# Scores by two sets of 64 rows in turn, in one two-bank tile, in the attention of a two-block transformer kernel

## The chip, the cores and the metric

The kernel runs on one NeuronCore of a Trainium2 chip. The metric is device time in microseconds (us), the median of the runs. The core has TensorE (PE, the matmuls; PEld are its weight loads), VectorE (DVE), ScalarE (ACT), GpSimdE (POOL) and SyncE (SP, which issues the DMAs). [...] Matmuls write to PSUM, which has eight banks of 128 partitions x 512 fp32.

## The reference, cut to what matters

The first block is a two-layer transformer on 512 tokens, the second block a single layer. The change lies in the attention of the first block, which has two kinds, run one after the other in each layer:

```python
# differential attention, 8 heads, two score sets of 64 features per head
sc = einsum('bhcqd,bhckd->bhcqk', q, k) * 64 ** -0.5     # c = 0, 1
p = softmax(sc)
w = p[:, :, 0] - lam * p[:, :, 1]
o = einsum('bhqk,bhkd->bhqd', w, v)                      # v: 128 features

# dilated windows, 3 groups x 4 heads of 64 features
sc = where(valid, q @ k^T * 64 ** -0.5, -1e30)
p = softmax over the keys of all three groups of a head  # joined by their log-sum-exp
o = p @ v                                                # v: 64 features
```

All inputs are fp32. Products are kept near fp32 by splitting a number into a high part in a shorter format (F32R) and a low part, the rest; a product is then hi*hi + hi*lo + lo*hi.

## The kernel before, in words

Each layer's `attention` is a list of six parts: four of kind A (differential, two heads `hl` each, parts j = 0 to 3) and two of kind B (dilated, two heads each, `half` 0 and 1). Part i+1 is projected (`project_a`, `project_b`) after part i's attention in program order, so projections and attention can run side by side. A scheduler sets the order on each engine by a cost model of its own and by priority in program order; the kernel pins a few instructions with `keep_in_program_order` (behind the matmul traced just before) and `issue_after`. q, k and v tiles have two buffers each, so a part's projection can be two parts ahead, not more.

Kind A: the score tile of 128 queries x 512 keys is made per head, query tile `qt` and set c. A set has 64 features, half of the array's rows. `stack` (L466 to L478) therefore lays q_hi and q_lo one above the other in 128 rows (`qst`), and k_hi twice (`kst`), so one full matmul (L495) gives hi*hi + lo*hi; a second one with 64 rows (L498) adds q_hi * k_lo (`tg`). The maximum (L536), the exponential (L539), the weighted difference (L544, L545), four transposes into a `ta` bank (L548), a copy to `wT` (L550) and four value products into the bank `pv` (L552) follow. The two sets' score tiles are two separate buffers of the tag `sc`, one bank each.

Kind B: per row block r (4) and head h (2), the scores of group 0 are made as in A (L609, L610) and those of groups 1 and 2 by two plain fp32 matmuls of 64 rows (L613) into a second `sc` bank. Mask adds (L616, L617), maximum, exponential (L622), scaling (L624), six transposes (L629) into two `ta` banks, two copies (L630, L631) and six value products (L635, 64 columns wide, into partitions 64h to 64h+63 of `pv`) follow. A plain fp32 matmul shows as two passes in the trace, an F32R one as one.

PSUM in the attention: `mm` 2 banks (projections), `tr` 1, `sc` 2, `ta` 2, `pv` 1. Around B half 1, four calls of `gates` (projections of the gate, two output tiles of 24 matmuls each) are traced early; two are free, two are held behind `self.b_ins[1]` and `[2]`, the last value products of r = 1 and r = 2.

## Time and profile before

| | before |
|---|---|
| median of 3 runs | 3705.43 us (3701.24 to 3707.47) |
| the profiled execution | 3702.62 us, span 3700.8 us |
| PE busy | 3565.2 us, 96% of the span |
| DVE / ACT / POOL busy | 71% / 42% / 21% |
| kind A attention of layer 0 | 109.85 to 354.7 us |
| kind B attention of layer 0 | 354.7 to 514.2 us |

The same two stretches of layer 1 run from 1075 to 1472 us. In a timeline row the first number is a start, the second how long the merged instructions took. A matmul's shown duration holds its pipeline's filling, so what one costs is the distance from its start to the next start. "64*128 64x512" is a matmul that uses 64 rows and 128 columns of the array on a moving operand of 512.

### The profile page before, as it was taken

To read this page: it belongs to the slowest core of one execution; us is meant where nothing else is said; L and a number is where in the kernel's file an instruction comes from. 1 tells how busy PE (TensorE), PEld (TensorE's weight loads), DVE (VectorE), ACT (ScalarE), POOL (GpSimd) and SP (SyncE) were. 2 spreads that over 40 slices of the span, in tenths; PEclk is the share of its full clock that TensorE was granted. 3 is DMA by queue.
4 is the path that set the end of the run, shared out by engine and by line. 5 is a ranking of instruction groups with operands and counts; after the bars stand their busy time and mean duration, and the time that the engine had idled before them with its cause. 6 is when DMAs were issued, how large, how long until landed. Compare 5 with 4: busy or idle time off the path is not lost.

```text
span 3700.8 us, 53078 instructions
## 1 busy us (share of the span) xinstructions
PE 3565.2 (96%) x19035; PEld 3036.2 (82%) x19035; DVE 2629.2 (71%) x6192; ACT 1558.3 (42%) x3041; POOL 781.3 (21%) x890
## 2 busy tenths in 40 slices
PE   6999999999999999999999999999998999999998
PEld 5888877988887888898887867899997888888887
DVE  7777568785378764468854575369999887777777
ACT  4566543423256654243243464433554333333332
POOL 4322200200142320020012220131101223333333
PEclk9999999999999999999999999999999999999999
DMA  5111247573321112345751111555455998888887
GB/s 194 64 41 52 69 134 258 173 248 123 110 78 46 56 45 66 100 158 191 241 162 59 54 55 41 164 171 171 159 201 199 335 332 291 299 301 292 297 300 277
DMA packets 228821, 611.33 MB, mean 165 GB/s; under 512 B 24070, under 2 KB 89638, under 8 KB 225868
## 3 DMA queue, kind: packets, MB, share of 16 engines
q1 hardware_dynamic: 191692, 473.69, 38.0%
q0 software_dynamic: 36864, 134.23, 10.8%
q8 instruction: 150, 2.46, 0.3%
q14 instruction: 115, 0.94, 0.1%
HBM read 566.66 MB, written 41.18 MB: 164 GB/s over the span
## 4 chain that ended last, share of the span: by engine, by line
PE 63%; DVE 15%; DMA 14%; ACT 4%; issue 3%; POOL 1%; DVEq 0%; ACTq 0%; SPq 0%; POOLq 0%
PE mm L124 14%; PE mm L125 14%; PE mm L126 14%; DMA raw<-uT 8%; DMA raw<-v 5%; DVE wlo L118 5%; ACT whi L117 3%; PE pv L552 2%; PE sc L498 1%; DVE oi L1770 1%; PE pv L635 1%; DVE adaj L229 1%; DVE oj L1762 1%; PE mm L1772 1%; PE sc L495 1%
## 5 line engine op out<-in xcount | busy, mean ns | idle before, releaser
L117 ACT CAST whi<-raw 128x1024 fp32r<-128x1024 f32 (+2 forms) x603 | 610.0, 1015 | 1160.0 <-DMA raw<-uT 398.8
L118 DVE TENSOR_TENSOR wlo<-raw,whi 128x1024 fp32r<-128x1024 f32 (+2 forms) x583 | 689.4, 1185 | 460.8 <-ACT whi L117 401.1
L126 PE MATMUL tr<-hhi,wlo 128*128 128x384 f32 x1024 | 353.8, 346 | 27.1 <-DVE wlo L118 27.0
L124 PE MATMUL mm<-hhi,whi 128*128 128x512 f32 (+1 forms) x976 | 365.9, 375 | 0.2 <-ACT mr L743 0.2
L125 PE MATMUL mm<-hlo,whi 128*128 128x512 f32 (+1 forms) x976 | 363.8, 373 | 1.8 <-DVE hlo L153 1.2
L126 PE MATMUL mm<-hhi,wlo 128*128 128x512 f32 (+1 forms) x976 | 363.9, 373 | 0.0
L124 PE MATMUL tr<-hhi,whi 128*128 128x384 f32 x1024 | 350.3, 342 | 13.8 <-ACT whi L117 10.7
L125 PE MATMUL tr<-hlo,whi 128*128 128x384 f32 x1024 | 347.2, 339 | 0.0
L124 PE MATMUL mm<-whi,hhi 128*128 128x384 f32 (+2 forms) x896 | 310.3, 348 | 18.7 <-ACT hhi L152 13.7
L125 PE MATMUL mm<-wlo,hhi 128*128 128x384 f32 (+2 forms) x896 | 310.8, 347 | 3.2 <-DVE wlo L118 3.2
L229 DVE CUSTOM_DVE_ANT_0 adaj<-adaw,cr 128x256 f32<-128x256 f32 x620 | 272.0, 439 | 58.7 <-DMA adaw<-ada_w 45.0
L126 PE MATMUL mm<-whi,hlo 128*128 128x384 f32 (+2 forms) x896 | 308.1, 344 | 0.0
L282 POOL TENSOR_TENSOR nsum<-nsum,nsq 128x256 f32<-128x256 f32 x78 | 68.6, 883 | 1114.5 <-ACT nsq L280 1113.0
L1845 POOL DMA_INDIRECT raw<-u,idx x128 | 148.4, 1159 | 457.3 <-DVE act L1853 315.2
L126 PEld LDWEIGHTS tr<-hhi,wlo 128*128 128x128 f32 x1024 | 194.1, 190 | 44.6 <-DVE wlo L118 43.6
L124 PEld LDWEIGHTS tr<-hhi,whi 128*128 128x128 f32 x1024 | 194.3, 190 | 26.9 <-ACT whi L117 21.1
L125 PEld LDWEIGHTS mm<-hlo,whi 128*128 128x128 f32 x976 | 183.8, 188 | 34.4 <-DVE hlo L153 1.6
L126 PEld LDWEIGHTS mm<-hhi,wlo 128*128 128x128 f32 x976 | 183.7, 188 | 32.9 <-issue 0.4
L124 PEld LDWEIGHTS mm<-hhi,whi 128*128 128x128 f32 x976 | 183.5, 188 | 32.5 <-issue 0.6
L124 PEld LDWEIGHTS mm<-whi,hhi 128*128 128x128 f32 x896 | 170.9, 191 | 38.4 <-ACT hhi L152 13.8
L125 PE MATMUL mm<-wlo,ewh 128*128 128x512 f32 x512 | 200.9, 392 | 0.0
L126 PE MATMUL mm<-whi,ewl 128*128 128x512 f32 x512 | 199.9, 392 | 0.0
(604 smaller groups left out, 8410.5 us busy)
## 6 DMA issues: line engine op xcount, KB each, us to landing
adaw<-ada_w SPq DMA_DIRECT2D x139, 512.0 KB, 4.4
raw<-uT SPq DMA_DIRECT2D x128, 512.0 KB, 4.6
raw<-v SPq DMA_DIRECT2D x128, 512.0 KB, 5.5
raw<-w_up SPq DMA_DIRECT2D x64, 512.0 KB, 4.3
raw<-w_dn SPq DMA_DIRECT2D x64, 512.0 KB, 3.6
raw<-w_b SPq DMA_DIRECT2D x48, 384.0 KB, 3.5
raw<-w_aqk SPq DMA_DIRECT2D x32, 512.0 KB, 3.7
raw<-w_g SPq DMA_DIRECT2D x32, 512.0 KB, 4.3
```

The costliest lines, as they stand in the source:

```text
L117: nc.scalar.copy(hi[:, :n], raw[:, :n])
L118: self.last_lo = (eng or nc.vector).tensor_sub(lo[:, :n], raw[:, :n], hi[:, :n])
L124: mm(ps, ah, bh, start=start, stop=False)
L125: mm(ps, ah, bl, start=False, stop=False)
L126: mm(ps, al, bh, start=False, stop=stop)
L229: nc.vector.tensor_tensor_reduce(junk, wt[:, q * 256 : q * 256 + 256], cond[:, q * 256 : q * 256 + 256], op0=ALU.mult, op1=ALU.add, scale= ...
L282: add_ins = (nc.vector if k == 7 else nc.gpsimd).tensor_add(tot, tot, sq)
L495: self.nc.tensor.matmul(ps, q(c, slice(0, P)), k(c), start=True, stop=False)
L498: self.nc.tensor.matmul(ps, q(c, r), k(2)[r], start=False, stop=True)
L552: nc.tensor.matmul(po[:, cols], wT[:, kt], v[:, kt, hl * P : hl * P + P], start=(kt == 0), stop=(kt == 3))
L635: ins = nc.tensor.matmul(po[rows, cols], v[:, kt, g * P + 64 * h : g * P + 64 * h + 64], wT[:, k, :], start=(k == 0), stop=(k == 5))
L1845: nc.gpsimd.indirect_dma_start(z, None, src, bass.IndirectOffsetOnAxis(ap=idx[:, k % P : k % P + 1], axis=0))
```

## The change

`stack`, `stack_one` and `stacked` go. `parts_of` makes the high and the low part of q and of k over all 128 partitions (set or head 0 in partitions 0 to 63, set or head 1 in 64 to 127), with one ACT and one DVE instruction. `three` lists the three 64-row products hi*hi, hi*lo, lo*hi of a score, and `by_turns` issues those of the two sets (A) or heads (B) alternately, each pinned behind the one before. The two scores of a turn lie in the two halves of one two-bank tile `pair` that has a single buffer, where there were two tiles of one bank. In B, both heads of an r go together: their scores, then the plain products of groups 1 and 2 (into `ta` banks now), later the value products of both heads alternately, once both `wT` are there.

```diff
     def attention_banks(self):
-        self.banks(mm=2, tr=1, sc=2, ta=2, pv=1)
+        self.banks(mm=2, tr=1, pair=1, ta=2, pv=1)
...
+        if tag == "sc" and "pair" in self.nbanks:
+
+            if not self.second_half:
+                self.second_half = [self.t(self.pm, [P, 2, 512], "pair")]
+                return self.second_half[0][:, 0]
+            return self.second_half.pop()[:, 1]
...
+    def by_turns(self, *products):
+
+        n = len(products[0])
+        for k in range(n):
+            for p, step in enumerate(products):
+                ins = self.nc.tensor.matmul(*step[k][:3], start=step[k][3], stop=step[k][4])
+                if k or p:
+                    self.tc.keep_in_program_order(ins)
+        return ins
+
+    def parts_of(self, hi, lo, src, gain):
+
+        self.nc.scalar.activation(hi, src, AF.Copy, scale=gain)
+        self.nc.vector.scalar_tensor_tensor(lo, src, gain, hi, ALU.mult, ALU.subtract)
+
+    def three(self, ps, q, k):
+
+        return [(ps, q[0], k[0], True, False), (ps, q[0], k[1], False, False), (ps, q[1], k[0], False, True)]
...
-                self.stacked(pss, lambda c, r: q[c][r, hl, cols], lambda c: k[c][:, hl])
+                self.by_turns(*(self.three(ps, [z[64 * c : 64 * c + 64, hl, cols] for z in q],
+                                           [z[64 * c : 64 * c + 64, hl] for z in k]) for c, ps in enumerate(pss)))
...
-            for h in range(2):
+            cols = slice(r * P, r * P + P)
+            pss = [(self.sc_ps(), self.bank("ta")) for _ in range(2)]
+            steps = []
+            for h, (ps, p2) in enumerate(pss):
                 rows = slice(64 * h, 64 * h + 64)
...
+                steps.append(self.three(ps, [qT[0][rows, i, cols] for i in range(2)], [kT[0][rows, i] for i in range(2)]))
+                steps[h] += [(p2[:, g * P : g * P + P], qT[1][rows, g, cols], kT[1][rows, g, cols], True, True)
+                             for g in range(2)]
+            self.by_turns(*steps)
...
+            ins = self.by_turns(*([(po[64 * h : 64 * h + 64, cols], v[:, k if k < 4 else r, 64 * (h + 2 * max(k - 3, 0)) :][:, :64],
+                                    wT[:, k, :], k == 4, k == 3) for k in (4, 5, 0, 1, 2, 3)] for h, wT in reversed(list(enumerate(wTs)))))
             self.b_ins = (self.b_ins if r else []) + [ins]
```

What the scheduler makes of it on PE, at the end of part j = 1 of kind A in layer 0, `hl` 1. Before (L495 and L498 are scores, `ta` transposes, `mm` projections):

```order
L495 MATMUL sc_1784<-kst_291_1186,qst_289_1184 128x512
L498 MATMUL sc_1784<-tg_1188,qst_289_1184 128x512
L125 MATMUL mm_2667<-wlo_2502,hhi_438 128x512
L495 MATMUL sc_1785<-kst_292_1187,qst_290_1185 128x512
L498 MATMUL sc_1785<-tg_1188,qst_290_1185 128x512
L563 MATMUL ta_1681<-ident_72,osb_1671 128x128 x4
L548 MATMUL ta_1709<-ident_72,p_1703 128x128 x4
L126 MATMUL mm_2667<-whi_2501,hlo_446 128x512
L124 MATMUL mm_2667<-whi_2501,hhi_439 128x512
L125 MATMUL mm_2667<-wlo_2502,hhi_439 128x512
L126 MATMUL mm_2667<-whi_2501,hlo_447 128x512
L124 MATMUL mm_2734<-whi_2724,hhi_432 128x256
```

And now, at the same part and head (L479 is `by_turns`, L541 the transposes, L545 the value products):

```order
L541 MATMUL ta_1671<-ident_72,p_1665 128x128 x4
L479 MATMUL pair_1716<-kst_281_1168,qst_279_1166 128x512 x2
L479 MATMUL pair_1716<-kst_282_1169,qst_279_1166 128x512 x2
L479 MATMUL pair_1716<-kst_281_1168,qst_280_1167 128x512 x2
L545 MATMUL pv_1649<-v_1386,wT_1676 128x128 x4
L541 MATMUL ta_1703<-ident_72,p_1697 128x128 x4
L545 MATMUL pv_1649<-v_1386,wT_1708 128x128 x4
L479 MATMUL pair_1748<-kst_281_1168,qst_279_1166 128x512 x2
L479 MATMUL pair_1748<-kst_282_1169,qst_279_1166 128x512 x2
L479 MATMUL pair_1748<-kst_281_1168,qst_280_1167 128x512 x2
L541 MATMUL ta_1735<-ident_72,p_1729 128x128 x4
L545 MATMUL pv_1649<-v_1386,wT_1740 128x128 x4
```

The projections that stood between the attention's steps have moved ahead of this place; here scores, transposes and value products follow each other with no projection between them, up to the next transposition of a projection (`tr`) and its matmuls.

On PE in kind B of layer 0, half 1, before (L635 are value products, `mm_4915` is a gate's projection):

```order
L124 MATMUL mm_4915<-hhi_432,whi_4911 128x512
L635 MATMUL pv_4538<-wT_4555,v_4409 64x128 x6
L629 MATMUL ta_4589<-ident_72,p_4578 128x128 x4
L629 MATMUL ta_4590<-ident_72,p_4578 128x128 x2
L609 MATMUL sc_4638<-kst_872_4183,qst_834_3965 128x512
L610 MATMUL sc_4638<-tg_3124,qst_834_3965 128x512
L613 MATMUL sc_4641<-kst_873_4184,qst_835_3966 128x128 x2
L125 MATMUL mm_4915<-hlo_440,whi_4911 128x512
L126 MATMUL mm_4915<-hhi_432,wlo_4912 128x512
```

And now, from the last value products of half 0 on (`pair_4559` are scores of half 1's r = 2, `ta_4426`, `ta_4427` and `ta_4493` plain products of its r = 0 and 1, L621 the transposes of its r = 0):

```order
L479 MATMUL pv_3604<-wT_3850,v_3475 64x128
L479 MATMUL pv_3604<-wT_3829,v_3475 64x128
L479 MATMUL ta_4427<-kst_831_4086,qst_793_3876 128x128
L479 MATMUL ta_4426<-kst_831_4086,qst_793_3876 128x128
L479 MATMUL ta_4427<-kst_831_4086,qst_793_3876 128x128
L479 MATMUL pair_4559<-kst_830_4085,qst_792_3875 128x512 x6
L621 MATMUL ta_4449<-ident_72,p_4438 128x128 x4
L621 MATMUL ta_4450<-ident_72,p_4438 128x128 x2
L621 MATMUL ta_4470<-ident_72,p_4459 128x128 x4
L621 MATMUL ta_4471<-ident_72,p_4459 128x128 x2
L479 MATMUL ta_4493<-kst_831_4086,qst_793_3876 128x128
L479 MATMUL pv_4424<-wT_4469,v_4295 64x128
```

The transposes of an r now stand right behind its plain products and the next scores, and the next r's plain products stand behind those transposes, since both use the two `ta` banks; the gates' projections stand before and after this stretch. The same two patterns stand in layer 1.

## Rows read from the trace of the kernel before

**Rows 1.** Busy time by stretch: kinds A and B, layer 0; then PEclk, DMA share, GB/s.

```profile
109.85:354.70 244.85, 244.33 (x1401) 200.18 (x1400) 191.35 (x457) 153.54 (x376) 77.45 (x107) 1.00 0.16 50
354.70:514.20 159.50, 159.50 (x918) 134.46 (x917) 84.72 (x168) 73.26 (x149) 23.68 (x41) 1.00 0.21 68
```

**Rows 2.** Chain of waits in kind B, 354.7 to 514.2 us, shares by line.

```profile
by line: PE mm L126 20.4%; PE mm L124 20.3%; PE mm L125 20.3%; PE pv L635 15.0%; PE ta L629 8.4%; PE sc L613 5.1%; PE sc L610 4.3%; PE sc L609 2.3%; PE tr L588 1.8%; PE pv L552 1.7%; PE ta L548 0.3%; PE ta L563 0.3%
```

**Rows 3.** Timeline of PE around one score of kind A: start, us, engine, line.

```profile
109.61 0.40 PE L126 MATMUL mm<-whi,hlo 128*128 128x512 f32 x1
109.85 0.39 PE L495 MATMUL sc<-kst,qst 128*128 128x512 f32 x1
110.17 0.49 PE L498 MATMUL sc<-tg,qst 64*128 64x512 f32 x1
110.59 0.50 PE L124 MATMUL mm<-whi,hhi 128*128 128x512 f32 x1
110.92 0.40 PE L125 MATMUL mm<-wlo,hhi 128*128 128x512 f32 x1
```

**Rows 4.** Timeline of PE where both sets' 64-row scores stand together, layer 1.

```profile
1136.60 0.49 PE L498 MATMUL sc<-tg,qst 64*128 64x512 f32 x2
1137.02 0.44 PE L511 MATMUL tr<-ident,qs 128*128 128x128 f32 x2
```

**Rows 5.** Timeline of PE in the second block, four plain products of 64x64, two passes each.

```profile
2093.13 0.66 PE L1479 MATMUL lm<-va,kw 64*64 64x129 f32 x8
```

**Rows 6.** Timeline of PE around the scores of one head of kind B.

```profile
472.61 0.50 PE L610 MATMUL sc<-tg,qst 64*128 64x512 f32 x1
472.94 0.60 PE L613 MATMUL sc<-kst,qst 64*128 64x128 f32 x4
473.48 0.50 PE L126 MATMUL mm<-hhi,wlo 128*128 128x512 f32 x1
```

**Rows 7.** Timeline of PE, value products of one head of kind B.

```profile
424.89 1.52 PE L635 MATMUL pv<-wT,v 128*64 128x128 f32 x12
```

**Rows 8.** Groups by line: one of the low parts in `stack`, DVE.

```profile
L476 DVE SCALAR_TENSOR_TENSOR qst<-tr,gcol,qst 64x256 fp32r<-64x256 f32 x26 | 12.6, 483 | 9.4 <-ACT kst L475 8.7
```

**Rows 9.** One line's instructions in kind A: duration ns min/median/max, first and last start.

```profile
L536 DVE TENSOR_REDUCE mx<-sc x128: 673/692/694, 110.9 to 1309.9; 128x1 f32<-128x512 f32 x128
L539 ACT ACTIVATE p<-sc,mx x128: 668/688/704, 112.5 to 1311.5; 128x512 f32<-128x512 f32 x128
L544 DVE TENSOR_SCALAR p<-p,s x64: 473/480/561, 117.9 to 1312.6; 128x512 f32<-128x512 f32 x64
L545 DVE SCALAR_TENSOR_TENSOR p<-p,s,p x64: 741/751/836, 119.4 to 1313.1; 128x512 f32<-128x512 f32 x64
L550 ACT COPY wT<-ta x64: 572/586/603, 126.8 to 1317.8; 128x512 f32<-128x512 f32 x64
```

**Rows 10.** Timeline of all engines, softmax of one head of kind B.

```profile
494.53 0.38 ACT L631 COPY wT<-ta 128x256 f32<-128x256 f32 x1
...
494.85 0.42 DVE L617 TENSOR_TENSOR p<-sc,mask 128x256 f32<-128x256 f32 x1 [2.87 <-PE sc L613]
...
495.31 0.95 DVE L619 TENSOR_REDUCE bmx<-p 128x1 f32<-128x768 f32 x1
495.31 0.39 PE L125 MATMUL mm<-hlo,whi 128*128 128x512 f32 x1
...
495.54 0.40 PE L126 MATMUL mm<-hhi,wlo 128*128 128x512 f32 x1
...
496.48 0.94 ACT L622 ACTIVATE p<-p,bmx 128x768 f32<-128x768 f32 x1 [1.58 <-DVE bmx L620]
...
497.74 0.62 DVE L624 TENSOR_SCALAR p<-p,bsum 128x768 f32<-128x768 f32 x1
```

**Rows 11.** Busy time by stretch around a wait of PE in the first projections.

```profile
60.30:63.80 3.50, 0.34 (x2) 0.00 (x0) 3.46 (x12) 0.92 (x1) 0.00 (x0) 1.00 0.25 74
63.89:67.30 3.41, 3.41 (x8) 2.69 (x9) 1.89 (x3) 1.14 (x2) 0.00 (x0) 0.50 0.58 180
```

## The prediction, made before the result was known

> **What bounds the kernel now.** I read the busy times by stretch first. In kind A of layer 0 PE is busy for 244.33 of 244.85 us, DVE for 191.35 (78%), ACT for 153.54; in kind B PE for all 159.50, DVE for 84.72 [rows 1]. The reader is to see that PE has no gap in either stretch, so what a score or value product costs on PE is paid in full, and what DVE or ACT does beside it is not. The chain of waits in B says the same: every share is PE's, the projections' three lines 61%, and the lines that the change touches (L609, L610, L613, L635) 2.3 + 4.3 + 5.1 + 15.0 = 26.7%, 42.6 us a layer [rows 2]. Then I read starts in the timeline to price a single score, and last the order on PE before and after, because a stretch that is full can only lose time if work stops lying beside the waits of the softmax.

> **PE work, kind A.** From the starts [rows 3]: a full score matmul is 0.32 to the next start (109.85 to 110.17), the 64-row one 0.42 (110.17 to 110.59), and the projection after it 0.33. Among projections alone it is 0.23 (495.31 to 495.54) [rows 10]. So the changes of shape cost 0.09, 0.19 (of which 0.11 is taken as a weight load that nothing hides, as the one behind shows) and 0.10, together 0.38, and a set costs two matmuls of 0.23 and that, 0.84; 1.68 a turn of two sets. After: six 64-row matmuls. Two 64-row matmuls that stand together take 0.42 to the next start (1136.60 to 1137.02), as long as one alone [rows 4]: the two sets use different halves of the rows and run side by side. So the turn costs 3 x 0.23 + 0.38, some 1.08; saved 0.60. There are 2 layers x 4 parts x 2 heads x 4 query tiles = 64 turns: **-38**. The other end: if they ran one after the other, 6 x 0.23 + 0.38 = 1.76, which is +5. I take the first, since rows 4 show that very pair.

> Whether the second and third pass of a set can load their weights while the set's own rows still work: four passes over the same 64 rows take 0.60, less 0.27 of emptying (what a matmul's shown 0.50 has over 0.23), so they stand 0.11 apart [rows 6], no further than twelve value products over all rows (1.52 less 0.27, over eleven) [rows 7]. I take no open load. [...]

> **PE work, kind B.** Per row block r and head: L609 0.32 as in A, L610 0.33 (472.61 to 472.94), L613 0.54 (472.94 to 473.48), and 0.11 on the matmul behind: 1.30 [rows 6]. Value products: twelve passes in 1.52 shown, 1.31 from the first to the next work's start (1.25 and one hand-over), and some 0.3 for the changes of shape around them [rows 7]. That is 2.9 a head, 5.8 for the two; the chain's 42.6 us over 8 row blocks is 5.3, which leaves out what the neighbours pay. After: scores 1.08, plain products of both heads side by side 4 x 0.11, together 1.5; value products of both heads by turns in 12 slots, 1.31, and 0.6 for changes: 3.4. Saved 2.4 x 16 (2 layers x 2 halves x 4) = **-38**. That half-column products of two heads run side by side is not shown here. The nearest row is of 64x64 passes: eight took 0.66 [rows 5], where one after the other would be 7 x 0.11 + 0.27 = 1.04. So pairs do run together. If the value products did not, 1.31 x 16 = 21 comes back.

> **Stacking.** Per 128 tokens of q and k, four ACT instructions, four low parts of 483 ns [rows 8] and two copies become two and two. Neither engine is the bound in A or B, and PE work lies over it, so nothing; the DMAs are the same. It matters only as room on DVE, rival 1.

> **What the order takes away.** PE now stands bare in some turns: no projection lies between a turn's steps. In B there are three such turns a layer (half 0's r = 3, half 1's r = 0 and 1), and r = 2 of half 0 has only fourteen projections (14 x 0.23 = 3.2 us). Their chain, with durations from [rows 10], from the last plain product on: 0.27 of emptying, two adds of 0.42, two maxima of 0.95 with 0.22 for the small operation and the hand-over behind each, the second exponential 0.94, 0.32 to the scaling, 0.62. The first head's scaling is squeezed in at about 4.2, its transposes (six at 0.11, and 0.27 of emptying) and copies (0.59 [rows 9], 0.38) end at 6.2. The `ta` banks are only two, and the plain products use them now as well: so the second head's transposes wait for those copies, the next r's plain products for the second head's copies (8.2), and with value products and plain products the turn closes at about 10.3. PE works for 1.1 (next scores) + 1.3 (transposes) + 1.3 to 1.6 (value products) + 0.4, some 4.5 in all; 5.8 idle. Per layer 3 x 5.8, 2.6 at the r with fourteen projections, and 1.3 (transposes' emptying and two copies) at each of the two last turns: 22.6, both layers **+45**. Behind the waiting transposes on PE stand the value products, the next scores and the gates' projections; all wait.

> In A the order has bare turns at the end of parts j = 0 (one), 1 (three) and 2 (three). `pair` has a single buffer, so the next scores wait for both exponentials. Chain of a turn, [rows 9] for durations: two maxima of 0.69 and their 0.2, exponential 0.69 and 0.19 for its sum, 0.47 for two small operations, 0.48, 0.75: 4.4. PE works for 1.08 + 0.44 + 0.44 and 0.4 of changes of shape, 2.4. So 2.0 idle in 7 turns, and at the end of each of three stretches a copy that the value products wait for (0.71 of transposes + 0.59): 18 a layer, **+36**. The ends: no idle at all, if the exponentials and DVE's steps of successive turns overlap fully, and 5.0 a turn (idle 2.6) if the copy to `wT` always stands ahead of the second exponential: 0 and 46.

> **Clock.** [...] The bare turns in B have one wait of about 3.1 us each: six, at some 1.4 us: **+8**; nothing at one end, 20 at the other, if the clock stays low through the whole of them.

> **Sum.** -38 - 38 + 45 + 36 + 8 = +13 on the profiled 3702.6 (the span 3700.8 and 1.8 around it): 3716. The median of the runs shown is 2.8 above the profiled one, so 3718.

> **Rivals.**
> 1. The other side: the A turns are not bare in effect. DVE without stacking has 3.3 us of work in a turn (2 x 0.84 + 0.48 + 0.75 + 0.33); if softmax steps of neighbouring turns overlap, a turn takes that, its idle is 0.8, and A's waits are 7 x 0.8 x 2 = 12 instead of 36: 3694. It decides from a turn under 3.5 us on, for then A wins more than B loses. For it: DVE is the next busiest engine in A and it gets lighter. Against: single-buffered `pair`. With B's turns also a quarter shorter, 3680.
> 2. Longer waits: the clock stays half through the bare stretches (+12) and an A turn takes 5.0 (+10, with the stretches' ends a little more): 3718 + 25 = 3743. For it: in B 3.1 us waits follow each other at 10 us. Against: between them PE works without a break for some us.
> 3. The change does not do what it says. Either each further pass over the same rows pays an open load of 0.11 [rows 3]: two in each of A's 64 turns, 14 us, and five in each of B's 16 row blocks, 9 us: 3741. Or the turns run one after the other: serial scores alone bring 44 in A, 3762; serial value products alone 21, 3739. Against: [rows 4 to 6]. [...]

> **How the numbers follow.** Forecast 0.50, with its own range 3696 to 3740 (waits of 81 us, give or take a quarter, and a little for the PE terms); rival 1 0.25; rival 2 0.17; rival 3 0.08 (0.05 for open loads, 0.03 for serial turns). A difference of 0.2%, 7.4 us, is about what a measurement of this kernel can tell from no change: 3698 to 3713. Of the forecast's half, 0.30 lies above 3713, 0.15 within, 0.05 below; rival 1 gives 0.22 faster and 0.03 within; rivals 2 and 3 are slower, but for 0.01. Faster 0.27, same 0.19, slower 0.54. The range takes in rival 1 from 3675 and rival 2 to 3750.

> **What would show it.** In the timeline of A, six L479 in about 1.08 us with starts in pairs, and in B value products of both heads starting in pairs; starts 0.23 apart singly would mean rival 3. Waits of PE of about 3 us ahead of L621 in B's bare turns, released by DVE's scaling, and of 1.3 ahead of the second head's, released by ACT's copy; a granted clock under 1.00 there. Stage B longer than its 159.5 us and A near its 245. I am wrong if A falls under 235 (rival 1) or if B, waits and all, stays under 155.

## The result, and the profile after

| | before | changed |
|---|---|---|
| median | 3705.8 us (3701.2 to 3707.5) | 3748.0 us (3746.8 to 3748.9) |
| ratio, 95% interval | | 1.0116 (1.0098 to 1.0133) |
| span of the profiled run | 3700.8 us | 3747.0 us |
| PE / DVE / ACT busy | 96% / 71% / 42% | 94% / 68% / 41% |

The changed kernel is 42 us slower. Each engine has less work than before; PE's 3541 us of it are spread over a span that is 46 us longer.

What the change was to save is there. The timeline of PE around one turn of kind A, in the kernel after (it answers to [rows 3]):

```profile
198.54 0.39 PE L131 MATMUL mm<-whi,hhi 128*128 128x512 f32 x1
198.86 0.98 PE L479 MATMUL pair<-kst,qst 64*128 64x512 f32 x6
199.76 0.50 PE L132 MATMUL mm<-wlo,hhi 128*128 128x512 f32 x1
```

Six passes take 0.90 us from their first start to the next work's, where the two sets took 1.56 before (49.8 us in layer 0 over 32 turns); their starts come in pairs (198.86, 199.20 and 199.44, twice each). What is new are waits of PE in an attention that had next to none [rows 1, 2]. Waits of PE in layer 0's attention, after (us in total, times, longest):

```profile
PE ta L621 <- DVE p L615: 10.9, 4, 3.7
PE pv L545 <- ACT wT L543: 5.5, 7, 1.2
PE mm L131 <- ACT sq L455: 3.7, 3, 1.5
PE ta L479 <- ACT wT L622: 2.7, 5, 1.3
PE pair L479 <- ACT p L532: 2.3, 2, 1.2
PE ta L621 <- ACT wT L622: 1.9, 4, 1.1
PE pv L479 <- ACT wT L623: 1.6, 1, 1.6
```

B's own (L621, L479 on `ta` and `pv`) sum to 17.1 us, A's (with 1.5 at `tr` and 1.4 at L541) to 10.7; the 3.7 ahead of projections (L131) were 0.5 in this layer before. In layer 1 each of these rows is the same within 0.5. Timeline of one bare turn of B, after, some rows left out:

```profile
452.17 0.48 PE L479 MATMUL ta<-kst,qst 64*128 64x128 f32 x2 [0.51 <-ACT wT L622]
452.59 2.76 PE L479 MATMUL pv<-wT,v 128*64 128x128 f32 x24
...
456.13 0.93 PE L479 MATMUL pair<-kst,qst 64*128 64x512 f32 x5
456.80 1.80 DVE L610 TENSOR_REDUCE bmx<-p 128x1 f32<-128x768 f32 x2
...
460.72 1.51 PE L621 MATMUL ta<-ident,p 128*128 128x128 f32 x6 [3.65 <-DVE p L615]
...
462.48 1.54 PE L621 MATMUL ta<-ident,p 128*128 128x128 f32 x6 [0.25 <-ACT wT L622]
...
464.33 0.79 PE L479 MATMUL ta<-kst,qst 64*128 64x128 f32 x2 [0.30 <-ACT wT L622]
```

The turn takes 12.16 us (452.17 to 464.33). The wait of 3.65 us for the softmax stands where the prediction put it, but what stands beside it is slow: six transposes take 1.51 us, and the 24 value products 2.76 here and 2.83 behind the wait (at 465.05), where those of an undisturbed turn take 1.53 (at 477.36). The granted clock says why: it was 0.52 from 452.59 to 455.40, and 0.50 from 459.60 to 469.70. Busy times by stretch (PE, PEld, DVE, ACT, POOL), then PEclk, DMA share, GB/s, after:

```profile
448.00:470.00 22.00, 15.83 (x103) 12.23 (x101) 10.89 (x22) 8.11 (x17) 0.00 (x0) 0.69 0.06 24
470.00:505.00 35.00, 26.95 (x154) 21.56 (x154) 14.70 (x33) 11.62 (x25) 0.00 (x0) 0.80 0.06 16
```

Where the time goes, by events that all kernels have (us later than in the kernel before; "layer 0's outputs" is the last matmul on `ohi` there, the last of the attention's output projection, "second block" its last `mm<-hhi,whi`, "end" the last matmul), with the median and its ratio of the kernels run. Each row's events are read from one profiled execution, which can lie several us off its median (5.6 above it for b_only, 5.5 below for after_fill). The kernels are those of the next section:

| | layer 0's outputs | layer 1's outputs | second block | end | median | ratio (interval) |
|---|---|---|---|---|---|---|
| changed | +7.2 | +27.8 | +36.3 | +47.5 | 3748.0 | 1.0116 (1.0098 to 1.0133) |
| two_sc | -0.4 | +9.0 | +9.6 | +24.6 | 3724.4 | 1.0054 (1.0037 to 1.0071) |
| a_only | -5.2 | -6.5 | -6.3 | -3.1 | 3699.7 | 0.9990 (0.9979 to 1.0002) |
| b_only | 0.0 | +12.8 | +16.5 | +26.6 | 3722.2 | 1.0047 (1.0030 to 1.0064) |
| serial | +12.2 | +42.0 | +42.1 | +46.5 | 3749.3 | 1.0125 (1.0107 to 1.0143) |
| after_fill | -2.4 | +11.0 | +13.5 | +14.6 | 3721.7 | 1.0043 (1.0029 to 1.0056) |
| after_warm | -1.4 | +14.6 | +16.6 | +20.4 | 3720.9 | 1.0039 (1.0020 to 1.0057) |
| after_qr | +6.6 | +29.6 | +32.0 | +38.7 | 3745.0 | 1.0110 (1.0090 to 1.0130) |
| by_turns_fill | -8.6 | -6.2 | -5.8 | -2.7 | 3703.9 | 1.0000 (0.9981 to 1.0018) |
| b_fill2 | -12.7 | -13.1 | -13.2 | -7.1 | 3695.3 | 0.9974 (0.9963 to 0.9986) |
| by_turns_fill2 | -17.7 | -22.9 | -22.5 | -19.0 | 3687.4 | 0.9959 (0.9946 to 0.9971) |
| a_rev | -7.1 | -10.3 | -9.8 | -2.9 | 3700.6 | 0.9994 (0.9981 to 1.0006) |

So 28 us of the loss arise in the first block, 8.5 in the second block's attention and 11 in the experts' part behind it, which goes on to the end and whose code is the same.

### The profile page after: what moved, and what is told of

Its sections match the earlier page's. It is cut to its first block, busy times and chain, and to the rows that moved or that the text cites. A ratio compares the mean times of both kernels' runs of the same rounds, so it can differ in the third digit from the quotient of the medians.

```text
span 3747.0 us, 53123 instructions
## 1 busy us (share of the span) xinstructions
PE 3540.9 (94%) x19195; PEld 3034.0 (81%) x19195; DVE 2565.4 (68%) x6000; ACT 1518.4 (41%) x2945; POOL 775.2 (21%) x890
## 4 chain that ended last, share of the span: by engine, by line
PE 61%; DVE 15%; DMA 15%; ACT 5%; issue 3%; POOL 1%; SPq 0%; DVEq 0%; ACTq 0%; POOLq 0%
PE mm L132 14%; PE mm L131 14%; PE mm L133 14%; DMA raw<-uT 8%; DVE wlo L125 5%; DMA raw<-v 3%; ACT whi L124 3%; PE pair L479 2%; PE pv L545 1%; DVE oi L1759 1%; PE mm L1761 1%; DVE ewl L160 1%; DMA act<-actd 1%; PE tr L133 1%; PE tr L131 1%
## 5 line engine op out<-in xcount | busy, mean ns | idle before, releaser
L131 PE MATMUL tr<-hhi,whi 128*128 128x384 f32 x1024 | 353.0, 345 | 15.7 <-ACT whi L124 10.2
L131 PE MATMUL mm<-hhi,whi 128*128 128x512 f32 (+1 forms) x976 | 366.0, 375 | 0.2 <-ACT mr L732 0.2
L131 PE MATMUL mm<-whi,hhi 128*128 128x384 f32 (+2 forms) x896 | 308.1, 345 | 24.8 <-ACT hhi L159 14.7
L131 PEld LDWEIGHTS tr<-hhi,whi 128*128 128x128 f32 x1024 | 196.4, 192 | 29.4 <-ACT whi L124 21.5
L131 PEld LDWEIGHTS mm<-hhi,whi 128*128 128x128 f32 x976 | 183.8, 189 | 32.5 <-ACT mr L732 0.4
L131 PEld LDWEIGHTS mm<-whi,hhi 128*128 128x128 f32 x896 | 170.7, 191 | 41.5 <-ACT hhi L159 15.0
```

The source lines that it names most:

```text
L131: mm(ps, ah, bh, start=start, stop=False)
```

## The experiments

**Which half of the change costs: two_sc, a_only, b_only.** In two_sc `pair` gives way to two buffers of one bank; a_only and b_only are the kernel before with one kind's functions exchanged.

```diff
-        self.banks(mm=2, tr=1, pair=1, ta=2, pv=1)
+        self.banks(mm=2, tr=1, sc=2, ta=2, pv=1)
```

> The changed kernel with the two-bank tile `pair` replaced by two tiles of one bank each (tag sc, two buffers, as before the change); scores and value products still go by turns. Theory (waits that the order leaves bare cost the time): the order now puts projections between all but 2 of the 64 turns of kind A, so A's extra idle of about 15 us a layer and the 4 us at the next layer's first outputs go, while kind B keeps its three bare turns a layer: 3690 to 3705. Rival (the time goes to the matmuls by turns themselves, or to code after the attention): 3735 to 3750.

> The kernel before with only kind A's scores by turns (two sc tiles of one bank, kind B as before). Theory: A's scores fall from 49.8 to about 30 us a layer, no bare turns are added in A or B, so 35 to 40 us are gained: 3665 to 3680. Rival (by turns itself brings waits to A): 3700 or more.

> The kernel before with only kind B changed (both heads together, plain products in the ta banks, value products by turns; two sc tiles of one bank, kind A as before). Theory: B saves about 13 us of PE work a layer, and its bare turns cost about 18 us of waits and 8 us of halved clock a layer: 3725 to 3740. Rival (all of the loss comes from the two-bank tile with its single buffer): 3675 to 3685.

Measured at layer 1's outputs: two_sc +9.0, a_only -6.5, b_only +12.8. The single buffer of `pair` therefore costs 19 us net, about half of what the theory put on it (15 a layer and 4), and B's half loses even without it. The medians still miss: two_sc by 20 us, 15 of which arise behind the second block's attention, b_only by 3 on the lower side, and A's half by 20, -6.5 instead of -35. With two banks the six passes of a turn rarely stand together. In two_sc, timeline of PE:

```profile
191.96 0.28 PE L133 MATMUL mm<-whi,hlo 128*128 128x256 f32 x1
192.17 0.50 PE L479 MATMUL sc<-kst,qst 64*128 64x512 f32 x1
192.60 0.39 PE L131 MATMUL mm<-whi,hhi 128*128 128x256 f32 x1
...
193.74 0.96 PE L479 MATMUL sc<-kst,qst 64*128 64x512 f32 x5
```

One pass goes alone and pays its change of shape (0.43 here), and the other five pay theirs (0.96 shown for five, where 0.98 are shown for six together); that this is because the first bank comes free ahead of the second is argued here, and a_rev tests it. From start to next start, a pass costs 0.211 us in a_only and 0.158 with `pair`: 40 us a layer in A against 30, after 50 before. The two-bank tile keeps the passes together and pays for it with waits. Nor does a_only keep the 10 us a layer that its scores save: in layer 0 its projections of 384 and 256 columns cost 2.8 us more than before, and A's transposes and value products 3.4 more; that this comes from the passes of another shape that they now stand next to is the author's reading.

**Does the first set matter: a_rev.** a_only with `reversed(list(enumerate(pss)))` in the call of `by_turns`.

> a_only with set 1 issued ahead of set 0 in each turn, so that fewer first passes stand alone between projections (34 turns of 64 split 1 and 5 in both, 25 runs of six instead of 16). Theory (a turn's six passes cost 0.21 us each with two banks and 0.16 with one two-bank tile because the first pass goes alone and pays its change of shape twice): a few us less than a_only, 3690 to 3698. Rival (the split does not matter): 3700.

The scores fall from 40.4 to 38.4 us a layer and layer 1's outputs come 4 us earlier than in a_only; 3700.6 against 3699.7 does not show it, since the trace loses it again in the experts' part: as the theory has it in the trace, inconclusive in the median.

**Does the alternation matter: serial.**

```diff
-        for k in range(n):
-            for p, step in enumerate(products):
+        for p, step in enumerate(products):
+            for k in range(n):
```

> The changed kernel with by_turns issuing all steps of the first set or head and then all of the second; the same matmuls, not alternated. Theory (two sets run side by side only when they alternate): 0.7 to 0.8 us more in each of 64 turns of A, 0.8 + 1.3 in each of 16 of B, some of it within the bare waits: 3790 to 3830. Rival (PE pairs neighbours in any order, or the alternation does nothing): 3748, as the changed kernel.

The median is that of the changed kernel, the rival's number, but by chance: at layer 1's outputs serial is 14 us later, and it gets that back because its second block does not lose the 8.5 us and its end loses less. The price per product was mis-expected all the same. Timeline of PE in serial, a turn of A and B's value products:

```profile
200.09 0.98 PE L479 MATMUL pair<-kst,qst 64*128 64x512 f32 x6
201.01 0.50 PE L132 MATMUL mm<-wlo,hhi 128*128 128x512 f32 x1
...
458.65 2.45 PE L479 MATMUL pv<-wT,v 128*64 128x128 f32 x24
```

Six score passes queued set by set still take 0.92 us, and A's scores cost 31.5 us a layer for 30.3. What grows are the 24 value products, from 1.53 (at the full clock, below) to 2.45 (granted clock 1.00).

**Waits against clock: after_fill and after_warm.** after_fill holds each output tile of the first four gates behind the value products of a row block (`self.b_ins` now keeps all eight of a layer); after_warm adds work.

```diff
-            for m, r in enumerate((None, None, 1, 2)):
+            for m, held in enumerate(((1, 2), (3, 4), (4, 5), (6, 6))):
```

```diff
+            if self.nth_b % 2 and r:
+                steps = [[(*z[0][:4], True)] * 12 + z for z in steps]
```

> The changed kernel with the eight output tiles of the first four gates' projections (24 matmuls, 5.5 us each) held one by one behind the value products of kind B's row blocks, so that projections stand in each of its formerly bare turns; kind A and the rest as in the changed kernel. Theory (bare turns: some 18 us of waits and 7 of halved clock a layer in B): 30 to 40 us less, 3708 to 3720, and a granted clock of 1.00 in that stretch. Rival (these waits only move to another place): 3740 to 3750.

> The changed kernel with work added: in half 1 of kind B, row blocks 1 to 3, the first score pass of both heads is issued 12 times more before the three that count (2.8 us more matmuls at the full clock in each of six turns, all ahead of the wait of 4 us for the softmax; the result is unchanged, since the last pass with start overwrites). Theory (the halved clock after the wait is a cost of its own, some 3 us a turn): the added passes hide in the wait, transposes and value products run at the full clock, 3725 to 3738. Rival (only the waits cost, the clock plays no part on this chain): 3746 to 3750. Third (the added passes themselves run at the half clock): 3755 to 3765.

after_warm is the plainest result of the study: 144 matmuls more, and 27 us less. 16 us of that lie in the two layers' attention (8.6 and 7.7, by the events; 3 of them are lost again behind layer 0's attention), 6 in the second block, the rest behind it. The same turn in after_warm:

```profile
452.56 0.48 PE L480 MATMUL ta<-kst,qst 64*128 64x128 f32 x2 [0.51 <-ACT wT L626]
452.98 1.53 PE L480 MATMUL pv<-wT,v 128*64 128x128 f32 x24
...
454.91 3.67 PE L480 MATMUL pair<-kst,qst 64*128 64x512 f32 x29
...
459.58 0.85 PE L625 MATMUL ta<-ident,p 128*128 128x128 f32 x6 [1.00 <-DVE p L619]
...
462.27 0.48 PE L480 MATMUL ta<-kst,qst 64*128 64x128 f32 x2 [0.51 <-ACT wT L626]
```

and its stretches:

```profile
448.00:470.00 22.00, 17.08 (x158) 13.35 (x156) 13.88 (x29) 10.51 (x24) 0.00 (x0) 1.00 0.08 25
470.00:505.00 35.00, 30.76 (x226) 24.96 (x225) 16.41 (x36) 13.47 (x28) 0.00 (x0) 1.00 0.07 20
```

The added passes fill the wait (1.00 is left of 3.65), the granted clock stays at 1.00, six transposes take 0.85 instead of 1.51, the value products 1.53 instead of 2.76, and the turn 9.71 instead of 12.16. The clock is a cost of its own, about as large as the theory said (2.5 us a turn for 3); the total gained more than expected, through the second block and what lies behind it. after_fill gains 17 us at layer 1's outputs, half of what was expected, and its median misses the range by 2: it left one turn bare (a wait of 5.9 us at 421 us, with a granted clock of 0.82 in 420 to 448 us), and the second heads' waits of 1.3 stayed.

**The second block: after_qr.**

```diff
+                with self.after(*(self.ropes[-3:-2] if (t, d) == (0, 1) else [])):
+                    for h in range(4):
+                        nc.scalar.activation(dm[:, h], dm[:, h], AF.Exp, bias=m[:, h : h + 1])
```

> The changed kernel with one order pinned in the second block: the first token tile's two rope copies (ACT, qR) stand ahead of the second direction's exponentials (dm), as they did in the kernel before. Theory (8 us of the loss are this order, which the scheduler's model of time shifted, and the half clock behind the wait of 2.0 us): 3738 to 3742, and the stretch from the second block's first lm matmul to its last mm<-hhi,whi about 386 us instead of 395. Rival (the clock falls there anyhow): 3746 to 3750.

In the changed kernel ACT has the copies to `qR` behind the exponentials of `dm`, where the kernel before has them ahead. Timeline of PE there, after, and then the same matmuls in after_qr and before:

```profile
2183.63 0.48 PE L1320 MATMUL th<-kTr,qR 64*128 64x256 f32 x1 [1.99 <-ACT qR L1224]
...
2198.86 2.07 PE L1319 MATMUL ms<-kTn,qT 128*128 128x512 f32 x2
2200.87 2.07 PE L1320 MATMUL ms<-kTr,qR 64*128 64x512 f32 x2
```

```profile
2185.13 0.48 PE L1321 MATMUL th<-kTr,qR 64*128 64x256 f32 x1 [1.72 <-ACT qR L1225]
...
2198.06 1.13 PE L1320 MATMUL ms<-kTn,qT 128*128 128x512 f32 x2
2199.12 1.12 PE L1321 MATMUL ms<-kTr,qR 64*128 64x512 f32 x2
```

```profile
2166.43 1.13 PE L1330 MATMUL ms<-kTn,qT 128*128 128x512 f32 x2
2167.49 1.12 PE L1331 MATMUL ms<-kTr,qR 64*128 64x512 f32 x2
```

From the first `lm<-whi,chi` matmul to the last `mm<-hhi,whi` it is 394.8 us after, 388.7 in after_qr, 386.4 before. The half clock of the later matmuls went with the order, 6 of the 8 us: the granted clock was 0.50 from 2193.50 to 2207.15 after, and 1.00 in after_qr from 2193.00 to 2206.70. The wait itself shrank little (1.99 to 1.72), so that this wait alone made the clock fall is not shown. Other kernels agree on the order: in two_sc and serial the copies to `qR` stand ahead of those exponentials, and they lose 0.6 and 0.1 us in this block. The median moved by 3 us, to between the two forecasts, and the two kernels' ranges overlap: confirmed in the stretch, not shown in the whole.

**A version that keeps the gain: by_turns_fill, b_fill2, by_turns_fill2.** by_turns_fill is two_sc with set 1 first and the gates held; in the other two a gate's tile is split, 15 matmuls behind a row block's value products and 9 behind the first head's transposes (`self.t_ins`), in b_fill2 with kind A as before.

```diff
-                    self.proj_feat(w, list(zip(hhi, hlo)), ps)
+                    b, split = held[n]
+                    for k in range(8):
+                        with self.after(*([] if b is None else [self.t_ins[2 * b + 2] if split and k > 4 else self.b_ins[b]])):
+                            self.mm3(ps, *w[k], hhi[k], hlo[k], k == 0, k == 7)
...
+            for m, held in enumerate((((1, 1), (2, 0)), ((2, 1), (3, 1)), ((4, 1), (5, 1)), ((6, 0), (6, 1)))):
```

> Both kinds by turns with two score tiles of one bank each, the set whose bank comes free last issued first (set 1), and the gates' projections held in kind B's bare turns as in after_fill. Theory: two_sc's 3724 less some 20 us of waits and clock in B, less a few us in A: 3695 to 3707. Rival (by turns with two banks keeps its cost through split turns and changes of shape wherever projections stand): 3715 to 3725.

> b_only (kind B by turns, kind A as before) with the gates' projections held so that every row block of B from the third on has 15 or more of their matmuls ahead of its first head's transposes and 9 between the two heads' transposes. Theory (by turns is cheaper on PE by some 13 us a layer in B, and only the bare turns hid it): 3722 less 16 us of waits and 7 us of halved clock a layer is 3676; with half of the waits left, 3690. Faster than the kernel before: 3676 to 3695. Rival (the gain of B's matmuls is lost in changes of shape once projections stand between them): 3703 to 3715.

> by_turns_fill with the same finer holding of the gates' projections as b_fill2 (in B, 15 matmuls ahead of the first head's transposes, 9 between the two heads'). Theory: some 6 us a layer less than by_turns_fill, whose third row block still waited 2.8 us and whose second heads 1.3: 3685 to 3695. Rival (what is left is changes of shape, not waits): 3700 to 3706.

by_turns_fill ends at the kernel before's time, within its expectation. by_turns_fill2 is faster than both kernels, 3687.4 us, inside its own; b_fill2 is faster than the kernel before too and lies at the upper end of its, for which half of the waits were to stay. Stretches of by_turns_fill2 for those shown above:

```profile
448.00:470.00 22.00, 19.41 (x129) 15.17 (x126) 12.79 (x26) 10.26 (x21) 0.00 (x0) 1.00 0.16 48
470.00:505.00 35.00, 29.87 (x199) 24.03 (x200) 16.06 (x30) 17.15 (x33) 0.00 (x0) 1.00 0.26 85
```

The clock no longer falls there; PE is busy for 19.4 of 22 us where it was for 15.8. By turns gains on PE, then, once each score has a bank of its own and the gates' projections stand in B's waits. The same holding of the gates on the kernel before was not run; its PE had no wait there to fill [rows 1].

## Why the prediction was right, and where it was short

Forecast 3718, slower, range 3675 to 3750; measured 3748, slower, near the upper end and outside the forecast's own narrower range of 3696 to 3740. By its steps, in us a layer, from starts to next starts in layer 0:

- *PE work of the scores and value products.* Scores 61.5 to 37.9, plain products 9.1 to 9.0, value products 24.1 to 15.6: 32 saved where 38 was forecast. The rest is the clock's: in after_warm plain products cost 7.2 and value products 11.8, and the saving is 38. Scores were right (0.90 a turn, or 1.10 with the 0.09 and 0.11 that the matmuls on either side take more, for 1.08), side by side as [rows 4] had shown.
- *Changes of shape.* Not in the forecast's PE work: A's transposes and value products, now next to scores of 64 rows and to waits, cost 12.0 + 27.8 before and 14.8 + 31.7 after, 7 more. From the start of a last value product it is 0.21 to a score's start, and 0.03 to a projection's.
- *Waits.* Forecast 22.6 in B and 18 in A; measured 17.1 and 10.7, in the places named, with the releasers named, and 3.2 more ahead of A's projections, which the forecast did not name. A's turns overlap more than the chain allowed: part of rival 1.
- *Clock.* This step was mis-sized. Forecast 8 for both layers, one slow stretch of 1.4 per turn, with 20 as the other end; after_warm shows 16. The 1.4 was the author's estimate, and no run shows it: the stretch in [rows 11] lasted 1.57 more than eight matmuls of 0.23, and the bare turn shown above 2.5 more than with the clock at 1.00. Behind the wait of 3.65 us the clock stayed at half through transposes and value products, as rival 2 had it. (Rival 2's longer A turns did not come: A waited less than forecast.) The wait alone does not settle when the clock falls: the first slow stretch, at 452.59, stands behind waits of 0.33, 1.12 and 0.51 only, and behind the same three it stayed at 1.00 in after_warm.
- *The sum ended with the attention.* Nothing was put down for code that is not touched. At layer 1's outputs the loss is 28 for a forecast of 13; 4 of it arise behind layer 0's attention, where PE waits once for DVE, and DVE for a load:

```profile
PE mm L131 <- DVE x L815: 3.5, 1, 3.5
```

```profile
DVE x L815 <- DMA x<-xT: 3.6, 1, 3.6
```

  The loads of `x` are issued on SP behind six loads of `w_up` now, 4.4 us ahead of their first use (647.11 to 651.50), where before they stood ahead of those loads and were 7.6 us early. Then come 8.5 in the second block (shown above) and 11 behind it. For the 11: the order there differs on PE, DVE and SP between kernels, and the same part lies 1 to 15 us over that of before in all of them; which difference makes it was not tried and stays open. Executions of the kernel before alone lie between 3697.8 and 3712.9 us, so a part of it may be no more than that.
- *The signs named.* Six passes in pairs, B's waits, their releasers and the clock came as named. The stages did not: from its first score to B's first, A took 275.2 us (105.62 to 380.86), and B, from there to its last value product, 143.7, which by the prediction's own words (under 155) would make it wrong. That sign took each stage to keep its work. But 130 projection matmuls of 384 columns (0.185 each, 24 us) that stood in B before stand in A's stretch now, and 11 of 512 (2.6 us) that stood ahead of A. With those in their old places A would have 248 and B 168: near its 245, and longer than its 159.5.

Added up as run, both layers: 63 saved, 13 for A's transposes and value products, 9 for B's transposes at the half clock, 61 for waits, 4 behind layer 0's attention, together 24 of the 28. So the mechanism was right, and that the sum came within 15 us there (30 at the end) is in part luck: waits were put 20 too high, while the clock, the neighbours and the untouched code were put too low.

Rival 3 fell: the trace has third passes 0.24 behind the second over the same rows (199.20 to 199.44), next to 0.23 for a projection, so no open load is paid there.

## What to carry to other kernels

Here cheaper matmuls paid as a whole only once other work lay between the attention's dependent steps (3687.4 us for by_turns_fill2, 3748.0 for the change alone): before merging two heads into one turn, decide what PE does during the one softmax chain that is left, and place it by hand. A wait of PE cost more than its length here: behind 3.65 us of it the granted clock was 0.50, and the 24 value products took 2.83 us instead of 1.53. And a change of one stage can move a scheduler's order behind it, so compare kernels by events along the program before reading the total.

## What the hardware showed that was not expected

144 matmuls that compute nothing new, put into six waits of 3.0 to 3.7 us, made the kernel 27 us faster; the granted clock rose from 0.69 and 0.80 to 1.00 in the stretches shown.
